# Encoder layer on one core: four regions of the schedule rewritten (opening, rotary tiles of the indexer, branch projections, last blocks)

## The chip, the cores and the metric

The kernel runs on one core of a Trainium2 chip. The metric is the device time of one execution in microseconds (us). Matrix products run on TensorE (PE in the profile), elementwise work on VectorE (DVE), ScalarE (ACT) and GpSimd (POOL); SyncE (SP) issues the transfers. A "split" below writes a float32 tile as a rounded high part (ScalarE) and the remainder as a low part (VectorE or GpSimd); each product is then three matmuls: high by high, high by low, low by high.

## The reference

One layer over 1024 positions of width 1024, in float32. Vectors of shift, scale and gain come from `mod = silu(c) @ w_ada + b_ada`. What is computed, cut to what matters here:

```python
h = rmsnorm(x) * (1 + sc1) + sh1
z = h @ w_in                      # q, k, v of three mixers, an indexer's qi, ki, wi, and the gates
yC: score = sum_h wi * relu(rope(qi_h) @ rope(ki)); top 256 keys per query; attention over them
merged = sum over 3 branches of sigmoid(gate_b) * (y_b @ w_branch[b])
x = x + g1 * rmsnorm(merged @ w_out)
u = gelu(conv(h2 @ w_up_a)) * (h2 @ w_up_g)
x = x + g2 * rmsnorm(u @ w_down)
```

## The kernel before

Positions lie in eight blocks of 128, channels in eight tiles of 128. Outside the parts that are ordered by hand, a planner with a model of the engines sets each engine's order and takes buffers from small pools as they come free; each engine then works strictly in that order. The names of pools are `k4`, `b4`, `e4`, `raw4`, `w4`, `p4` (seven, seven, five, three, four and twelve buffers of 4 KB a partition).

**Opening** (lines 275 to 384, by hand on four engines). SyncE loads the weights of the first modulation pair (`ada_in[0]`), the eight blocks of x, the indexer's weights `raw_qi`, the pair `ada_in[1]`, the keys' weights `raw_kk`, and further pairs. `x_norm(t)` (L299) does a block's square sum on ScalarE, its rsqrt on GpSimd and its scaling on VectorE, all before the next block's. Then for each channel tile k: transposes of x on TensorE (`g0_turn`), modulation and high part on ScalarE (`g0_hi`), low part on GpSimd (`g0_lo`), 18 matmuls into three output tiles (`g0_mm`: two of the indexer's queries, one of keys), while VectorE forms the eight products of the next pair's modulation weights with c (`ada_steps`, 128x256 each, L196, L198). `ada_end` adds the halves, has TensorE sum over the partitions (L208) and writes shift and scale of the next tile (L210), without which `g0_hi` of that tile can't run.

**Rotary tiles** (L394 to L434). `rope` copies a tile out of the banks (ScalarE), has four transfers exchange its halves into `zs`, multiplies z by cos on VectorE (L402), zs by sin on GpSimd (L403) and adds on VectorE (L404): first two query tiles, then the keys' tile. `stack_k` then splits the keys and copies them to the other half of the partitions by transfers (L419, L420); the scores of the indexer (L426, L429) need both copies. Beside this TensorE has 48 matmuls for a mixed tile (L247 to L249, `pm`) and 192 of 128x256 for mixer A's values (L470 to L472), the first of the *fill items*, which the planner sets wherever TensorE would be free. The values' weights are split when the first fill item begins, in `w4` buffers that the mixed tile's weights `wm2` and the indexer's also use.

**Branches** (L992 to L1030). For each branch b and channel tile m, a 128 KB piece of `w_branch` is loaded and split (L1002 to L1004), a gate tile is loaded, 12 matmuls go into two banks of three (L1017 to L1019), VectorE multiplies by the gate (L1021), and for b > 0 GpSimd adds to `M` (L1023). The two y tiles of a branch are loaded and split when the branch begins (L997, L998).

**Last blocks** (L1599 to L1624). The down projection runs in five rounds of seven products into eight banks (`XB`, `VB`), added to `acc` by VectorE (`down_add`, L1643). The last two weight rows are done apart: `final_block(tb)` has 12 matmuls into two banks, and VectorE adds them to `acc` (L1615), ScalarE squares (L1616), GpSimd multiplies by the gain (L1617), then the norm (L1619, L222, L224), and VectorE adds to x (L1623) and SyncE stores. The even blocks go after product 4 of the last round and the odd ones after product 6.

## Time and profile before

| | |
|---|---|
| runs | 1581.08, 1584.87, 1584.56 us; median 1584.56 |
| profiled execution, its own time | 1577.21 us |
| its span | 1575.4 us |
| TensorE, VectorE, ScalarE, GpSimd busy | 95, 73, 50, 36% of the span |

All times of the trace count from the start of the span. An engine's row says in brackets how long it sat idle before the instruction and what released it. The granted clock is a share of TensorE's upper level of 2.4 GHz, so 0.5 is its lower level of 1.2 GHz; a mean between tells how much of a stretch was at either.

### The profile page before, as it was taken

Reading aid. Unit: us, or ns where it says so; the run is one execution under the profiler, and the core shown is the slowest. Engines: PE = TensorE matmul, PEld = TensorE weight load, DVE = VectorE, ACT = ScalarE, POOL = GpSimd, SP = SyncE. Lnnn points to the kernel's source line nnn. Section 1 sums busy time; section 2 is a strip of 40 time slices with the busy share of each in tenths; the row PEclk is TensorE's granted clock in tenths of the full one; section 3 lists DMA queues with packets and bytes.
Section 4 is the critical chain, followed back from the end, with each engine's and each line's share of the span. In section 5 each row is a group of like instructions: output and inputs, shape, how many; then the busy total and the mean of one; then the engine's idle time right before and its main releaser. Section 6 shows DMA issues by size and latency. Waiting matters only on the chain.

```text
span 1575.4 us, 21143 instructions
## 1 busy us (share of the span) xinstructions
PE 1493.3 (95%) x7322; PEld 1234.4 (78%) x7322; DVE 1157.1 (73%) x2106; ACT 787.0 (50%) x1462; POOL 559.6 (36%) x396
## 2 busy tenths in 40 slices
PE   3989999999998999998999989999999999999996
PEld 2878888887887788776888778788888887788885
DVE  6665888998559755557536779888778777879868
ACT  4434698886554444532235455555555554522222
POOL 3632544343443443205542323222223222323305
PEclk9999999999999999999999999999999999999999
DMA  9541332344443452346666412444444445898762
GB/s 287 137 107 47 105 111 84 124 129 131 122 132 90 121 160 88 111 150 204 217 265 215 142 54 94 170 158 166 152 146 164 153 148 173 329 354 293 280 227 108
DMA packets 181727, 253.98 MB, mean 161 GB/s; under 512 B 14891, under 2 KB 132851, under 8 KB 181619
## 3 DMA queue, kind: packets, MB, share of 16 engines
q1 hardware_dynamic: 181619, 252.62, 48.3%
q8 instruction: 58, 0.95, 0.3%
q14 instruction: 50, 0.41, 0.1%
HBM read 169.75 MB, written 74.97 MB: 155 GB/s over the span
## 4 chain that ended last, share of the span: by engine, by line
PE 69%; DVE 15%; DMA 5%; issue 4%; ACT 4%; SPq 2%; POOL 1%; DVEq 0%; POOLq 0%; ACTq 0%
PE g L247 4%; PE g L248 4%; PE X L1268 4%; PE g L249 4%; PE X L1269 4%; PE X L1270 4%; PE X L1632 2%; PE X L1633 2%; PE X L1634 2%; PE V L1268 2%; PE V L1269 2%; PE V L1270 2%; PE V L1632 2%; PE V L1633 2%; PE V L1634 2%
## 5 line engine op out<-in xcount | busy, mean ns | idle before, releaser
L669 ACT ACTIVATE junk<-sc,thr 128x512 bf16<-128x512 f32 (+2 forms) x93 | 80.1, 861 | 25.6 <-DVE thr L690 19.7
L671 DVE TENSOR_SCALAR_CACHE_REDUCE junk<-sc,thr 128x384 bf16<-128x384 f32 (+2 forms) x93 | 89.8, 966 | 1.9
L1234 POOL TENSOR_TENSOR T<-ua 128x512 f32<-128x512 f32 x21 | 27.2, 1294 | 175.7 <-DVE rT L1220 166.1
L1312 POOL TENSOR_TENSOR cv<-cv,g 128x1024 f32<-128x1024 f32 x22 | 57.1, 2598 | 49.3 <-ACT cv L1311 35.4
L1269 PE MATMUL X<-left_S,rT 128*128 128x512 f32 (+1 forms) x184 | 70.8, 385 | 0.2 <-DVE left_S L1114 0.2
L1268 PE MATMUL X<-left_S,rT 128*128 128x512 f32 (+1 forms) x184 | 70.8, 385 | 0.0
L1270 PE MATMUL X<-left_S,rT 128*128 128x512 f32 (+1 forms) x184 | 70.7, 384 | 0.0
L1522 ACT ACTIVATE T<-work 128x512 fp32r<-128x512 f32 x40 | 25.0, 631 | 63.2 <-PE V L1634 26.1
L1235 POOL TENSOR_TENSOR ug<-ug 128x512 f32<-128x512 f32 x22 | 33.0, 1501 | 65.2 <-DVE ua L1228 65.2
L1643 DVE TENSOR_TENSOR acc<-acc,X 128x512 f32<-128x512 f32 x68 | 45.7, 683 | 13.6 <-PE X L1634 13.3
L1023 POOL TENSOR_TENSOR M<-M,tgb 128x1024 f32<-128x1024 f32 x12 | 30.6, 2567 | 66.0 <-DVE tgb L1021 62.2
L585 DVE SCALAR_TENSOR_TENSOR ada_acc<-ada_row,c_act,ada_acc 128x512 f32<-128x512 f32 x42 | 39.3, 936 | 12.9 <-DMA ada_row<-in_w_ada 12.4
L1633 PE MATMUL X<-T,ring 128*128 128x512 f32 x120 | 47.0, 392 | 0.0
L1634 PE MATMUL X<-T,ring 128*128 128x512 f32 x120 | 46.7, 390 | 0.0
L1632 PE MATMUL X<-T,ring 128*128 128x512 f32 x120 | 46.2, 393 | 0.0
L1643 DVE TENSOR_TENSOR acc<-acc,V 128x512 f32<-128x512 f32 x56 | 37.3, 682 | 11.6 <-PE V L1634 11.1
L1220 DVE TENSOR_TENSOR rT<-ua,rT 128x512 fp32r<-128x512 f32 x45 | 38.7, 861 | 9.3 <-ACT rT L1219 9.0
L1219 ACT ACTIVATE rT<-ua 128x512 fp32r<-128x512 f32 x45 | 28.2, 627 | 33.0 <-DVE ua L1232 22.6
L1220 DVE TENSOR_TENSOR rB<-ua,rB 128x512 fp32r<-128x512 f32 x44 | 40.8, 931 | 2.0 <-ACT rB L1219 0.9
L1269 PEld LDWEIGHTS X<-left_S,rT 128*128 128x128 f32 x184 | 34.5, 187 | 8.0 <-DVE left_S L1114 0.4
L1270 PEld LDWEIGHTS X<-left_S,rT 128*128 128x128 f32 x184 | 34.5, 187 | 7.7
L637 DVE SCALAR_TENSOR_TENSOR sc<-rl,wi,sc 128x512 f32<-128x512 f32 (+3 forms) x30 | 30.2, 1038 | 14.0 <-ACT rl L636 14.0
(988 smaller groups left out, 5559.8 us busy)
## 6 DMA issues: line engine op xcount, KB each, us to landing
ring<-L_spill SPq DMA_DIRECT2D x70, 512.0 KB, 6.0
L_spill<-S SPq DMA_DIRECT2D x40, 512.0 KB, 4.0
L_spill<-A SPq DMA_DIRECT2D x30, 512.0 KB, 3.1
raw_g<-in_w_in SPq DMA_DIRECT2D x24, 512.0 KB, 4.1
ada_row<-in_w_ada SPq DMA_DIRECT2D x24, 512.0 KB, 4.0
ua<-in_w_up SPq DMA_DIRECT2D x22, 512.0 KB, 4.3
ug<-in_w_up SPq DMA_DIRECT2D x22, 512.0 KB, 3.9
gate_spill<-tg SPq DMA_DIRECT2D x20, 512.0 KB, 2.7
```

Source lines behind the costliest of these rows:

```text
L247: pe.matmul(o, wh[:, k], hh[:, k, ts_], start=(k == 0), stop=False)
L248: pe.matmul(o, wh[:, k], hl[:, k, ts_], start=False, stop=False)
L669: act.activation(junk_a[:, 0:n], scores[b], AF.Sign, scale=-1.0, bias=t_f, accum_out=cnt[:, j:j + 1])
L671: dve.tensor_scalar(junk_d[:, 0:n], scores[b], t_f, None, op0=OP.is_lt, op1=OP.add, accum_out=cnt[:, j:j + 1])
L1220: eng.tensor_tensor(hl_[1], src, hl_[0].bitcast(F32), op=OP.subtract)
L1268: pe.matmul(oc, r[:, 0, k], lh, start=(first and k == 0), stop=False, skip_group_check=True)
L1269: pe.matmul(oc, r[:, 0, k], ll, start=False, stop=False, skip_group_check=True)
L1270: pe.matmul(oc, r[:, 1, k], lh, start=False, stop=(last and k == 3), skip_group_check=True)
L1632: pe.matmul(o, lh, r[:, 0], start=(starts and k == 0), stop=False, skip_group_check=True)
L1633: pe.matmul(o, lh, r[:, 1], start=False, stop=False, skip_group_check=True)
L1634: pe.matmul(o, ll, r[:, 0], start=False, stop=(k == 1), skip_group_check=True)
L1643: dve.tensor_tensor(dst, dst, banks[i], op=OP.add)
```

## The change

- **Opening.** The square sum and rsqrt of block t now go before the scaling of block t-1; the second weight tile `wqi1` and the pair `ada_in[1]` come on VectorE right after `wqi0`, and the keys' weights are split on GpSimd before the loop over k. From channel tile 2 on, the modulation comes in three *quads* of four column groups (2 MB each, eight transfers, rows of 1 KB in place of 512 B): eight products of 128x512, half of them in each of two steps or all eight in one. `g0_lo` follows `g0_hi`, and at k = 0 the low products of m = 0 and 1 go ahead of the modulation sum.
- **Rotary tiles.** The indexer's three tiles multiply by sin on VectorE too; the order is query tile 0, keys, `stack_k`, query tile 1. `wm2` lies in `b4`. The weights of A's values are loaded and split (high on ScalarE, low on GpSimd) ahead of the rotary tiles.
- **Branches.** `w_branch` comes in six groups of 512 KB, each split in one pair of instructions one group ahead; the y tiles of branch b+1 are loaded at m = 2 and split at m = 4 and 6; those of branch 0 and the first group stand ahead of the loop. `p4` has thirteen buffers.
- **Last blocks.** The last rows' products of the odd blocks' first half and the even blocks' second half are summed in the bank that the down projection still holds, so one VectorE addition does for two; the odd blocks' steps interleave with product 6, by hand on three engines; the very last half is multiplied by the gain on VectorE, all others on GpSimd, as before.

```diff
-N_RAW, N_E, N_K4, N_B4, N_STK, N_PT, N_BI, N_P4 = 3, 5, 7, 7, 4, 2, 1, 12
+N_RAW, N_E, N_K4, N_B4, N_STK, N_PT, N_BI, N_P4 = 3, 5, 7, 7, 4, 2, 1, 13
...
-YG_POOL = (2, 2, 2, 2, 2, 2, 2, 1)
...
+    def ada_quad_load(t, alloc):
+        wv = w_ada.rearrange("(k p) c -> p k c", p=P)
+        raw = [alloc[g](f"ada_quad{t}_{g}", (P, 2, 4 * P)) for g in range(4)]
+        for g in range(4):
+            for j, c in enumerate((t, 8 + t)):
+                nc.sync.dma_start(raw[g][:, :, j * 2 * P:(j + 1) * 2 * P], wv[:, 2 * g:2 * g + 2, c * P:(c + 2) * P])
+        return [raw[k // 2][:, k % 2] for k in range(KD)]
+    def ada_quad_steps(acc, per_k):
+        for k in range(KD):
+            if k == 0:
+                dve.tensor_scalar(acc, per_k[k], c_act[:, k:k + 1], None, op0=OP.mult)
+            else:
+                dve.scalar_tensor_tensor(acc, per_k[k], c_act[:, k:k + 1], acc, op0=OP.mult, op1=OP.add)
+            yield acc
+    def ada_quad_end(t, acc):
+        pm = bank("n", "ada_ps")
+        for j in range(4):
+            pe.matmul(pm[:, j:j + 1], acc[:, j * P:(j + 1) * P], one, start=True, stop=True)
+        for j, c in enumerate((t, t + 1, 8 + t, 9 + t)):
+            last = dve.scalar_tensor_tensor(mod[:, c:c + 1], pm[:, j:j + 1], mod_b1[:, c:c + 1],
+                                            mod_g[:, c:c + 1], op0=OP.add, op1=OP.mult)
+        return last
...
+    quads = {2: ada_quad_load(2, [k4_any] * 4)}
-    for k in range(2, 4):
-        ada_in[k] = ada_load((k, 8 + k), k4_any if k % 2 == 0 else raw4)
+    quads[4] = ada_quad_load(4, [raw4, raw4, raw4, b4])
+    quad_acc = b4("quad_acc", (P, 2, 4 * P))
...
-    def x_norm(t):
-        ss = sm(f"ss{t}")
-        act.activation(junk_a, xn[t], AF.Square, accum_out=ss)
-        r = rstd_of(ss, f"r{t}")
-        dve.tensor_scalar(xn[t], xn[t], r, None, op0=OP.mult)
+    x_r = {}
+    def x_square(t):
+        x_r[t] = sm(f"ss{t}")
+        act.activation(junk_a, xn[t], AF.Square, accum_out=x_r[t])
+    def x_rstd(t):
+        x_r[t] = rstd_of(x_r[t], f"r{t}")
+    def x_scale(t):
+        dve.tensor_scalar(xn[t], xn[t], x_r[t], None, op0=OP.mult)
...
+    quad_of = {}
+    def quad_go(t, n):
+        if t not in quad_of:
+            quad_of[t] = [ada_quad_steps(quad_acc[:, t // 2 % 2], quads[t]), None]
+        for _ in range(n):
+            quad_of[t][1] = next(quad_of[t][0])
     with tc.manual_schedule(engines={E.Activation, E.DVE, E.Pool, E.PE}):
-        for t in range(6):
-            x_norm(t)
-        g0_turn(0, 0)
+        for t in range(NB - 1):
+            x_square(t)
+            x_rstd(t)
+            if t:
+                x_scale(t - 1)
+            if t == 4:
+                g0_turn(0, 0)
-        for t in range(6, NB):
-            x_norm(t)
+        x_square(7)
+        x_rstd(7)
+        x_scale(6)
+        x_scale(7)
-        wqi(1, pool)
+        wqi(1, dve)
+        g0.append(split(raw_kk, (P, KD, P), "wkk", pool, lambda n, sh: f4(n, F32R, sh)))
+        for acc in ada_steps(ada_in[1]):
+            pass
         for k in range(KD):
+                    g0_lo(k, hf)
+            if k == 2:
+                quads[6] = ada_quad_load(6, [k4_any] * 4)
-                steps = ada_steps(ada_in[k + 1])
-                if k:
-                    for n, acc in enumerate(steps):
-                        if n in (3, 5):
-                            g0_lo(k, n // 4)
-                else:
-                    for acc in steps:
-                        pass
-                    g0.append(split(raw_kk, (P, KD, P), "wkk", pool, lambda n, sh: f4(n, F32R, sh)))
-                if k + 4 < KD:
-                    ada_in[k + 4] = ada_load((k + 4, 12 + k), k4_any if k % 2 == 0 else raw4)
-            else:
-                for hf in range(2):
-                    g0_lo(k, hf)
-            if k + 1 < KD:
-                start_end = ada_end((k + 1, 9 + k), acc, eng=dve)
+            if k == 0:
+                g0_mm(k, 0, True)
+                g0_mm(k, 1, True)
+                start_end = ada_end((1, 9), acc, eng=dve)
+                quad_go(2, 4)
+            elif k in (1, 3, 5):
+                if k < 3:
+                    quad_go(k + 1, 4)
+                start_end = ada_quad_end(k + 1, quad_of[k + 1][1])
+            elif k in (2, 4):
+                quad_go(k + 2, 8)
-            for m in range(3):
+            for m in range(2 if k == 0 else 0, 3):
...
-    wm2 = split(raw_m[:, :, 0:72], (P, KD, 72), "wm2")
-    def rope(halves, name, scale, alloc):
+    wm2 = split(raw_m[:, :, 0:72], (P, KD, 72), "wm2", alloc=b4r)
+    def v_weights(c0, name, alloc):
+        ws = []
...
+        return ws
+    va_weights = v_weights(C_VA, "va", w4)
+    def rope(halves, name, scale, alloc, eng=pool):
...
-        pool.tensor_tensor(zs, zs, sin, op=OP.mult)
+        eng.tensor_tensor(zs, zs, sin, op=OP.mult)
...
-    z_qi = [rope(g0_ps[m], f"qi{m}", 1.0, b4) for m in range(2)]
-    z_kk = rope(g0_ps[2], "kk", 1.0, k4)
+    def idx_q(h):
+        return stack_q(b4r, z_qi[h // 2], (h % 2) * 64, f"qi{h}")
+    z_qi = [rope(g0_ps[0], "qi0", 1.0, b4, dve)]
+    z_kk = rope(g0_ps[2], "kk", 1.0, k4, dve)
+    k_idx = stack_k(b4r, z_kk, 64, "ki")
+    z_qi.append(rope(g0_ps[1], "qi1", 1.0, b4, dve))
...
+    def branch_y(b):
+        raws = []
+        for j in range(2):
+            raws.append(k4(f"yb{b}_{j}"))
+            nc.sync.dma_start(raws[j], y_spill[b, j])
+        n_y = iter(range(4))
+        def place(n, sh):
+            i = next(n_y)
+            return p4r(n, sh) if b == 1 and i else e4(n, sh, F32R)
+        def steps():
+            for j in range(2):
+                y_next.append(split(raws[j], (P, S), f"y{b}_{j}", alloc=place))
+                yield
+        return steps()
+    def branch_w(g):
+        rb = raw4(f"wbr{g}", (P, 2, HALF))
+        nc.sync.dma_start(rb, w_branch[g // 2][:, g % 2 * HALF:(g % 2 + 1) * HALF].rearrange("(k p) c -> p k c", p=P))
+        return split(rb, (P, 2, HALF), f"wb{g}", alloc=w4 if g < 4 else p4r)
+    y_next = []
+    for _ in branch_y(0):
+        pass
+    wb_next = branch_w(0)
     for b in range(3):
-        y_s = []
-        for j in range(2):
-            yt = k4(f"yb{b}_{j}")
-            nc.sync.dma_start(yt, y_spill[b, j])
-            y_s.append(split(yt, (P, S), f"y{b}_{j}", alloc=lambda n, sh: e4(n, sh, F32R)))
+        y_s, y_next = y_next, []
         for m in range(KD):
-            wb = p4r(f"wb{b}_{m}", (P, 2, 2, P))
-            rb = raw4(f"wbr{b}_{m}", (P, 2, P))
-            nc.sync.dma_start(rb, w_branch[b][:, m * P:(m + 1) * P].rearrange("(k p) c -> p k c", p=P))
-            act.activation(wb[:, 0], rb, AF.Copy)
-            dve.tensor_tensor(wb[:, 1], rb, wb[:, 0].bitcast(F32), op=OP.subtract)
+            if m % 4 == 0:
+                wb = wb_next
+            elif m % 4 == 1 and (b < 2 or m < 4):
+                wb_next = branch_w(b * 2 + m // 4 + 1)
+            if b < 2:
+                if m == 2:
+                    y_steps = branch_y(b + 1)
+                elif m in (4, 6):
+                    next(y_steps)
+            mc = slice(m % 4 * P, (m % 4 + 1) * P)
...
-    def final_block(tb, banks):
...
+    class Final:
+        def __init__(self, tb):
+            self.tb, self.i, self.odd = tb, tb // 2, tb % 2
+            self.xr = (e4 if tb % 3 else raw4)(f"xf{tb}")
+            nc.sync.dma_start(self.xr, x1_spill[tb * P:(tb + 1) * P, :])
+            self.ss2 = sm(f"n3_{tb}ss2", 2)
+            self.y, self.yg = acc[:, tb], work[:, 4 + self.i]
+        def half(self, e, o, start):
+            for k in range(2):
+                l, r = fin[k][0][self.odd], fin[k][1][e]
+                lh, ll = (l[:, j, self.i * P:(self.i + 1) * P] for j in range(2))
+                pe.matmul(o, lh, r[:, 0], start=(start and k == 0), stop=False, skip_group_check=True)
+                pe.matmul(o, lh, r[:, 1], start=False, stop=False, skip_group_check=True)
+                pe.matmul(o, ll, r[:, 0], start=False, stop=(k == 1), skip_group_check=True)
+            y = self.y[:, es]
+            dve.tensor_tensor(y, y, o, op=OP.add)
+            sq = small.tile([P, HALF], F32, tag="ada_acc", name=f"sq{self.tb}", bufs=1)
+            act.activation(sq, y, AF.Square, accum_out=self.ss2[:, e:e + 1])
+        def gained(self, e):
+            y = self.y[:, es]
+            (dve if e and self.tb == NB - 1 else pool).tensor_tensor(self.yg[:, es], y, G2[e], op=OP.mult)
+        def norm(self):
+            ss = sm(f"n3_{self.tb}ss")
+            dve.tensor_tensor(ss, self.ss2[:, 0:1], self.ss2[:, 1:2], op=OP.add)
+            self.r = rstd_of(ss, f"n3_{self.tb}")
+        def end(self, halves=(0, 1)):
+            tb, xr, r = self.tb, self.xr, self.r
+            for e in halves:
+                es = slice(e * HALF, (e + 1) * HALF)
+                dve.scalar_tensor_tensor(xr[:, es], self.yg[:, es], r, xr[:, es], op0=OP.mult, op1=OP.add)
+                nc.sync.dma_start(out[tb * P:(tb + 1) * P, es], xr[:, es])
...
+                if c == N_C - 1 and n == 4:
+                    final_operands()
+                    evens = [Final(2 * i) for i in range(4)]
+                elif c == N_C - 1 and n == 6:
+                    odds = [Final(2 * i + 1) for i in range(4)]
+                    loads.enter_context(tc.manual_schedule(engines={E.Activation, E.DVE, E.Pool}))
                 for i, _ in enumerate(down_mm(n, next_ops())):
-                    down_add(n, i)
+                    if c < N_C - 1 or n not in (4, 6):
+                        down_add(n, i)
+                    elif n == 4:
+                        evens[i].half(1, VB[i], False)
+                        evens[i].gained(1)
+                    else:
+                        odds[i].half(0, XB[i], False)
+                        if i:
+                            odds[i - 1].norm()
+                        odds[i].gained(0)
+                        odds[i].half(1, VB[i], True)
+                        if i == 3:
+                            odds[3].gained(1)
+                            odds[3].norm()
+                        if i:
+                            odds[i - 1].end()
+                        if i < 3:
+                            odds[i].gained(1)
+                if c == N_C - 1 and n == 6:
+                    odds[3].end()
+                    loads.close()
...
-            if c == N_C - 1:
-                if n == 4:
-                    final_operands()
-                    for i in range(4):
-                        final_block(2 * i, VB[i % 2 * 2:i % 2 * 2 + 2])
-                elif n == 6:
-                    for i in range(4):
-                        final_block(2 * i + 1, (VB if i < 2 else XB)[i % 2 * 2:i % 2 * 2 + 2])
+            if c == N_C - 1 and n == 4:
+                for i in range(4):
+                    evens[i].half(0, VB[i], True)
+                    evens[i].gained(0)
+                    evens[i].norm()
+                    evens[i].end()
```

## Rows read from the trace of the kernel before

**Rows 1.** The page: busy time of the engines over the span, with share and instructions

```profile
PE 1493.3 (95%) x7322; PEld 1234.4 (78%) x7322; DVE 1157.1 (73%) x2106; ACT 787.0 (50%) x1462; POOL 559.6 (36%) x396
```

**Rows 2.** Windows: TensorE, its weight loads, VectorE, ScalarE, GpSimd busy; granted clock; DMA share, GB/s

```profile
26.00:41.00 15.00, 10.29 (x35) 7.70 (x34) 13.61 (x21) 5.13 (x7) 8.88 (x5) 1.00 1.13 264
79.00:125.00 46.00, 39.89 (x247) 34.16 (x246) 28.57 (x31) 16.26 (x28) 14.88 (x5) 0.93 0.36 92
125.00:175.00 50.00, 50.00 (x246) 42.51 (x245) 35.89 (x52) 21.85 (x41) 20.08 (x13) 1.00 0.31 87
175.00:350.00 175.00, 169.44 (x976) 144.98 (x974) 160.33 (x432) 152.88 (x335) 77.30 (x67) 1.00 0.34 102
475.00:525.00 50.00, 43.84 (x219) 35.99 (x220) 48.43 (x90) 20.12 (x40) 18.88 (x13) 0.90 0.30 86
688.00:752.00 64.00, 57.02 (x240) 44.47 (x239) 43.63 (x59) 15.10 (x29) 23.46 (x10) 0.97 0.63 201
1550.00:1575.40 25.40, 13.57 (x60) 10.79 (x58) 19.43 (x35) 5.79 (x16) 11.94 (x12) 0.87 0.34 125
```

**Rows 3.** Timeline, opening: start, length, instructions [idle before, releaser]

```profile
23.46 1.75 DVE L303 TENSOR_SCALAR x<-x,r7r 128x1024 f32<-128x1024 f32 x1 [0.66 <-POOL r7r L224]
25.13 3.38 DVE L232 TENSOR_TENSOR wqi0l<-raw_qi,wqi0h 128x1024 fp32r<-128x1024 f32 x1
28.43 3.74 DVE L196 TENSOR_SCALAR ada_acc<-ada_raw,c_act 128x256 f32<-128x256 f32 x2
...
36.17 0.34 DVE L210 SCALAR_TENSOR_TENSOR mod<-ada_ps,mod_b,mod_g 128x1 f32<-128x1 f32 x2 [1.17 <-PE ada_ps L208]
...
40.85 0.48 PE L333 MATMUL g_0a<-hh,wqi0h 128*128 128x512 f32 x1
```

**Rows 4.** Timeline, TensorE's modulation sums of two successive steps of the opening

```profile
48.28 0.50 PE L208 MATMUL ada_ps<-one,ada_acc 128*128 128x1 f32 x4
...
53.77 0.50 PE L208 MATMUL ada_ps<-one,ada_acc 128*128 128x1 f32 x4
```

**Rows 5.** The page, group: one 128x512 modulation sum on VectorE (count, busy, mean ns)

```profile
L585 DVE SCALAR_TENSOR_TENSOR ada_acc<-ada_row,c_act,ada_acc 128x512 f32<-128x512 f32 x42 | 39.3, 936 | 12.9 <-DMA ada_row<-in_w_ada 12.4
```

**Rows 6.** Waits of TensorE in 20 to 79 us: total, times, longest

```profile
PE ada_ps L208 <- DVE ada_acc L204: 4.0, 2, 3.2
```

**Rows 7.** Waits of TensorE in 79 to 125 us

```profile
PE ix L426 <- DVE qi L412: 3.3, 1, 3.3
PE vaps L471 <- POOL va1l L232: 2.9, 1, 2.9
```

**Rows 8.** Timeline, rotary tiles and first index scores

```profile
84.13 1.23 DVE L402 TENSOR_TENSOR z_qi<-z_qi,cos 128x1024 f32<-128x1024 f32 x1 [6.38 <-DMA zs_qi<-z_qi]
87.66 3.41 DVE L404 TENSOR_TENSOR z_qi<-z_qi,zs_qi 128x1024 f32<-128x1024 f32 x1 [2.31 <-POOL zs_qi L403]
...
98.94 1.23 DVE L404 TENSOR_TENSOR z_kk<-z_kk,zs_kk 128x1024 f32<-128x1024 f32 x1
...
109.46 0.86 PE L429 MATMUL ix<-ki,qi 128*128 128x512 f32 x3
```

**Rows 9.** Waits of TensorE in 688 to 752 us

```profile
PE yp L1017 <- DVE tgb L1021: 3.6, 3, 1.8
PE yp L1017 <- ACT wb L1003: 1.9, 2, 1.4
```

**Rows 10.** Groups in 690 to 752 us: the low parts of the branch weights

```profile
L1004 DVE TENSOR_TENSOR wb<-wbr,wb 128x256 fp32r<-128x256 f32 x20 | 16.5, 832 | 8.9 <-ACT wb L1003 8.9
```

**Rows 11.** Timeline, the tail

```profile
1563.17 0.40 PE L1614 MATMUL X<-wl,ring 128*128 128x512 f32 x1
...
1565.20 0.68 DVE L1615 TENSOR_TENSOR acc<-acc,X 128x512 f32<-128x512 f32 x1
1565.91 1.45 DVE L1617 TENSOR_TENSOR work<-acc,G 128x512 f32<-128x512 f32 x1
...
1570.81 1.41 DVE L1623 SCALAR_TENSOR_TENSOR xf<-work,n_7r,xf 128x512 f32<-128x512 f32 x2 [0.66 <-POOL n_7r L224]
```

## What I predict for the changed kernel

> **What bounds the kernel now.** I read the page first, then windows by stage, then in each stage that the change touches the waits of TensorE and the timeline around them. TensorE is busy 1493.3 of 1575.4 us [rows 1]; the other engines have far more slack over the whole. So only the 82.1 us without a matmul, and stretches at a lowered clock, can be won, as long as TensorE is full afterwards. The windows show where they lie [rows 2]: an unfinished opening (26 to 41: 4.7 us idle), the rotary stretch 79 to 125 (6.1 us idle, mean clock 0.93), the branches 688 to 752 (7.0 us, 0.97), the end. In 125 to 175 TensorE is busy 50.00 of 50 us: what is won before it is passed on and not absorbed there. The profiled execution took 1577.21 us, 7.35 us under the median of the runs; I form the sum as a difference on the trace and take it off the median of 1584.56.
>
> **Opening.** VectorE has the chain. The last scaling of x took 1.75 us, the low part of the first weight tile 3.38 [rows 3], where an operation of that size with nobody beside takes 1.23 [rows 8]: GpSimd was on its own split meanwhile. The change orders the norms so that a block's rsqrt runs under another's scaling (worth 0 to 1.75 us; I take 1.0) and does both weight tiles on VectorE, 2 x 1.23 = 2.5 us. The modulation products then begin at 25.13 - 1.0 + 2.5 = 26.6 in place of 28.43: 1.8 us. Their first two took 3.74 us [rows 3]; a product of twice that width takes 0.94 [rows 5], so unblocked two are at most 1.9. The keys' low part still runs on GpSimd and moves ahead, so of the 1.9 I take 1.5 (0 to 1.9). From the shift and scale at 36.17 to the first matmul of k = 1 at 40.85 there are 4.7 us [rows 3] with ten matmuls and four transposes; four of the ten now go before, about 1.4 (0 to 1.9). That is 4.7 us at k = 1. The steps after it are 53.77 - 48.28 = 5.49 us each [rows 4], TensorE's own work, and stay. Of the two waits for a modulation sum of 4.0 us together the longer, 3.2, is part of this; the other 0.8 [rows 6] was late weights and goes, since quad 6 is asked for at k = 2. Against: the quads. The queue already moves 264 GB/s at a full share (1.13) [rows 2], and 2.1 MB instead of 1.05 MB must land before step k = 2, up to 2.1 / 0.264 - 1.05 / 0.264 = 4.0 us later. On SyncE the bias loads, cos, sin and the mixed tile's weights queue behind eight more issues per quad; their readers come tens of us later, which hides that; without that cover it is the same 4.0. I take 0.5 of the 0 to 4.0. VectorE's work fits: eight products of 0.94 [rows 5] are 7.5 us per two steps of 11.0. Sum: 4.7 + 0.8 - 0.5 = 5.0 us, bounds 0 and 8.
>
> **Rotary tiles and values.** TensorE waits twice in 79 to 125: 2.9 us for the low part of the values' second weight tile, 3.3 us for the indexer's first query split [rows 7]. These are the 6.1 us; the clock of 0.93 adds 7% of 46, 3.2 us [rows 2]. Both waits come out of VectorE and GpSimd sharing a stage: an addition took 3.41 us beside GpSimd's multiplication, and the cos product 1.23 without it [rows 8]. With sin on VectorE the query and keys' tiles are six operations of 1.23: from 84.13 the keys are ready at 91.5 in place of 98.94 + 1.23 = 100.2, 8.7 us sooner, and the second score product, after the same transfers, at about 100.8 instead of 109.46 [rows 8]. Till then TensorE has the mixed tile and the values. The values' splits now stand on GpSimd ahead of the rotary tiles, while VectorE sits idle 6.38 us for the exchange [rows 8]; that hides them, and without it the 2.9 stays. Moving `wm2` costs two of seven `b4` buffers: the copy of query tile 1 out of its banks may wait on ScalarE until tile 0's `zs` is done, 84.13 + 3 x 1.23 = 87.8, and the splits of the keys are queued behind it; they can't begin before 91.5 anyway, so 0 (3.7 at most). The planner writes TensorE's order from modelled times, so I let 1.3 of the second wait and 0.8 of the clock's loss stay: 6.1 + 3.2 - 2.1 = 7.2, taken as 7 us, bounds 2.9 and 9.3.
>
> **Branches.** 7.0 us idle and 3% of 64, 1.9 us, by the clock [rows 2]: 8.9. Of the waits 1.9 us are for a weight's high part and 3.6 for VectorE's emptying of a bank [rows 9]. VectorE's small splits, 20 in this stretch, took 16.5 us, 0.83 each [rows 10]; six of four times the size are 6 x 1.23 alone or 6 x 3.41 beside GpSimd [rows 8], 7 to 20 us, so VectorE gains little and may lose, but they are asked for four tiles ahead. So the 1.9 goes, and most of what I don't have named, while half of the 3.6 and of the clock's 1.9 stays, with 1.0 for the last attention products ahead: 8.9 - 1.8 - 0.9 - 1.0 = 5.2, taken as 5 us, bounds 2 and 8. SyncE loses 18 issues; the y tiles' loads move ahead in its queue by some tiles, past gate loads that are needed later.
>
> **Last blocks.** The last matmul begins at 1563.17 and ends at 1563.57, 11.8 us before the end. The last addition begins only at 1565.20, and after the norm the last pair of results at 1570.81 for 1.41 us [rows 11], 3.2 us before the end: VectorE had four halves queued. With blocks interleaved, behind the last matmul stand an addition (0.68), the gain (1.45), two one-column sums (I estimate 0.3), the former block's pair and the last pair (1.41 each): 5.4, with the 3.2 it is 8.6, so 3.2 us less; 3 taken. The rsqrt on GpSimd hides under the former block's pair. If the gain took 0.68 as an addition does, 4.0 would be won. Eight additions fewer are off the path. Product 4 now needs the last rows' tiles 6 us or so sooner; no row shows when these land, so 0, with up to 1.5 as bound. Bounds 1 and 4.
> The gain took 1.45 us with a multiplication on GpSimd beside it [rows 11]. The Trainium skill, "SBUF — State Buffer", section "Who interferes with whom", says that a VectorE instruction with two SBUF inputs and a GpSimd one that reads SBUF shut each other out for a whole instruction; the row agrees. It speaks against this part, for GpSimd keeps fifteen of sixteen gains while VectorE's pairs move beside them: with one more such block behind the last matmul the saving would be about 2 us instead of 3.
>
> **Sum.** 5 + 7 + 5 + 3 = 20 us: the profiled execution would go from 1577.2 to 1557.2, the median from 1584.6 to 1564.6.
>
> **Rivals.**
> *The planner keeps the waits.* Rotary stretch and branches are not ordered by hand: if the scores stand as early in TensorE's order as now, or the banks are emptied as late, only opening and tail remain, 8 us: 1576.6. For it: both waits of rows 7 are of an order that time did not bear out. Against: four causes of waits go from the data's side. Chance 0.17.
> *Given back later.* In 175 to 350 VectorE is busy 160.3 of 175 us [rows 2]; if the search for thresholds there, and not TensorE, sets when attention can go on, what opening and rotary tiles win becomes idle time of TensorE: 8 us from branches and tail, 1576.6. Against: TensorE has 169.4 of 175, and the scores come earlier as well. Chance 0.07.
> *Slower.* In 475 to 525 VectorE is full (48.43 of 50), TensorE idles 6.2 us and the clock of 0.90 takes 5.0: 11.2 us per 50 [rows 2]. The planner's new times reorder the 500 us of fill behind the opening. If 175 to 350 became like that, it would lose 3.5 x 11.2 - 5.6 (idle already) = 33.6 us: 1598. It decides from the point at which VectorE lacks its 14.7 us of slack there, that is, fill items used up before. Against: the change adds no VectorE work after 100 us, and the rates that hand out fill are as they were. Chance 0.05.
>
> **How the numbers follow.** The forecast holds with 0.66, 1551 to 1572; 0.05 for still more (all upper ends: 1555, with a lucky reorder less). Opening, rotary, branches and tail at their lower ends, 0 + 2.9 + 2 + 1, give 1578.7. The range 1550 to 1578 takes in the forecast and most of the first two rivals. A measurement tells about 0.3% from no change, 4.8 us: faster than 1579.8 are the forecast, the better case and most of the two rivals, 0.89; 0.06 within, 0.05 slower.
>
> **What would show it.** Right: the first matmul of k = 1 near 36, the opening's end some 5 us earlier, no wait for a modulation sum over 1 us; the rotary stretch without the values' wait, and scores 13 us earlier with the opening's 5; six weight splits in the branches and under 4 us idle; less than 9 us behind the last matmul. Wrong: a wait for quad weights at k = 2, sin products slower than 1.3 us, or new idle time of TensorE over 10 us between 125 and 688, which would be the planner's and overturn the sum.

## The result, and the profile after

The median of the runs is 1568.01 us after (1564.69 to 1569.83) against 1583.85 before (1581.08 to 1584.87); the ratio is 0.9902, 95% interval 0.9883 to 0.9921. The forecast of 1564.6 was 3.4 us too low, and faster was right: 20 us were forecast, 15.8 came. But the parts of the sum did not come as they were forecast: the branches gave more, the last blocks nothing, the opening nothing against its own profile, and the stretch behind the rotary tiles took some back. The profiled execution of after took 1564.69 us (span 1562.6), 12.5 less than that of before.

Part 1 of the page of after (busy time, share, instructions):

```profile
PE 1490.3 (95%) x7322; PEld 1233.8 (79%) x7322; DVE 1131.3 (72%) x2054; ACT 783.4 (50%) x1444; POOL 547.9 (35%) x392
```

TensorE's time without a matmul fell from 82.1 to 72.3 us. A table by stage shows where the rest lies. The marks are first matmuls before which the same work has been done in each kernel (but for two matmuls of some 1240 at the first mark): mixer A's third score tile (`A2s`), mixer C's last (`C3s`), the output projection (`wo`) and the down projection (`X`).

| from the profiles, us | before | after | after - before |
|---|---|---|---|
| start to A2s (opening, rotary tiles, scores) | 260.4 | 251.7 | -8.7 |
| A2s to C3s (search, attention, gates) | 384.9 | 388.4 | +3.5 |
| C3s to wo (branches) | 164.8 | 156.1 | -8.7 |
| wo to X | 101.6 | 102.0 | +0.4 |
| X to the end | 663.7 | 664.4 | +0.7 |

The stretches of after that answer to [rows 2] (stretch, its length, then busy time and count of each engine, granted clock, DMA share, GB/s):

```profile
25.00:41.00 16.00, 12.75 (x43) 9.72 (x42) 14.62 (x19) 5.29 (x7) 6.80 (x4) 0.79 0.99 302
79.00:125.00 46.00, 45.21 (x298) 39.73 (x297) 29.03 (x49) 19.50 (x32) 9.54 (x4) 1.00 0.40 104
674.00:752.00 78.00, 76.54 (x358) 63.07 (x357) 43.33 (x58) 21.49 (x28) 33.68 (x14) 1.00 0.58 200
```

The rotary stretch and the branches are full at the full clock; the opening is not. TensorE's waits in the second and third of these stretches, all of them, in answer to [rows 7] and [rows 9] (total, times, longest):

```profile
PE ix L485 <- DVE sc L683: 0.5, 1, 0.5
PE vaps L525 <- ACT va L528: 0.3, 1, 0.3
...
PE yp L1096 <- DVE M L1100: 0.8, 1, 0.8
PE yp L1097 <- DVE y_1l L258: 0.7, 1, 0.7
```

The opening of after, in answer to [rows 3] (start, duration; in brackets the idle time before and what ended it):

```profile
26.80 1.64 DVE L195 TENSOR_SCALAR ada_acc<-ada_raw,c_act 128x256 f32<-128x256 f32 x2
28.36 4.56 DVE L197 SCALAR_TENSOR_TENSOR ada_acc<-ada_raw,c_act,ada_acc 128x256 f32<-128x256 f32 x6
29.46 2.38 POOL L258 TENSOR_TENSOR wkkl<-raw_kk,wkkh 128x1024 fp32r<-128x1024 f32 x1 [1.44 <-ACT wkkh L257]
...
33.52 0.98 PE L207 MATMUL ada_ps<-one,ada_acc 128*128 128x1 f32 x4 [3.22 <-DVE ada_acc L203]
...
34.54 0.34 DVE L209 SCALAR_TENSOR_TENSOR mod<-ada_ps,mod_b,mod_g 128x1 f32<-128x1 f32 x2 [1.17 <-PE ada_ps L207]
...
35.31 7.29 DVE L233 SCALAR_TENSOR_TENSOR quad_acc<-ada_quad,c_act,quad_acc 128x512 f32<-128x512 f32 x7
...
38.63 0.71 PE L366 MATMUL g_0a<-hh,wqi0h 128*128 128x512 f32 x1
...
42.75 1.02 PE L239 MATMUL ada_ps<-one,quad_acc 128*128 128x1 f32 x8 [1.78 <-DVE quad_acc L233]
...
46.82 0.48 PE L366 MATMUL g_0a<-hh,wqi0h 128*128 128x512 f32 x1
```

The first row shows the products beginning at 26.80, as worked out (26.6). The next two show GpSimd's split of the keys beside the six later products, which take 4.56 us. TensorE waits 3.2 us for their sum as it did before, its next matmuls take 0.63 to 0.78 us in place of 0.39, and k = 1 begins at 38.63. Then it waits 1.8 us for the first quad, and k = 2 begins at 46.82, later than the 46.34 of before.

The rotary chain of after, in answer to [rows 8], and the view of the tile with the second score product (min/median/max ns, first and last start):

```profile
90.32 1.23 DVE L461 TENSOR_TENSOR z_qi<-z_qi,cos 128x1024 f32<-128x1024 f32 x1 [18.06 <-DMA zs_kk<-z_kk]
...
96.24 1.22 DVE L463 TENSOR_TENSOR z_kk<-z_kk,zs_kk 128x1024 f32<-128x1024 f32 x1
...
L488 PE MATMUL ix<-ki,qi x15: 280/393/397, 104.9 to 125.8; 128*128 128x512 f32 x10, 128*128 128x384 f32 x3, 128*128 128x256 f32 x1, 128*128 128x128 f32 x1
```

Every operation takes 1.2 us, as forecast, but VectorE begins at 90.32 and not at 84.13. The row names the keys' exchange as what ended the wait, but the last transfer of that lands only at 92.4; the first query tile's, which the operation needs, lands at 90.1. The first score product begins at 104.7 us (104.27 before) and the second kind at 104.9 (109.46 before), 4.6 us sooner where 13 had been named as the sign. The last blocks, in answer to [rows 11]:

```profile
1549.84 2.96 POOL L1705 TENSOR_TENSOR work<-acc,G 128x512 f32<-128x512 f32 x2
1549.90 3.44 DVE L1716 SCALAR_TENSOR_TENSOR xf<-work,n_3r,xf 128x512 f32<-128x512 f32 x2
...
1550.72 0.40 PE L1695 MATMUL V<-wl,ring 128*128 128x512 f32 x1
1553.26 0.67 DVE L1698 TENSOR_TENSOR acc<-acc,X 128x512 f32<-128x512 f32 x1
...
1554.82 1.77 DVE L1705 TENSOR_TENSOR work<-acc,G 128x512 f32<-128x512 f32 x1
...
1556.78 1.41 DVE L1716 SCALAR_TENSOR_TENSOR xf<-work,n_5r,xf 128x512 f32<-128x512 f32 x2
```

When the last matmul runs, VectorE is in a pair of results that takes 3.44 us beside GpSimd's two gains (the same pair without GpSimd: 1.41, last row). Behind the last matmul stand 1562.6 - 1551.12 = 11.5 us; before it was 11.8.

### The profile page after: what moved, and what is told of

The parts are those of the page before. It is cut to its first block, busy times and chain, and to the rows that moved or that the text cites. A ratio compares the mean times of both kernels' runs of the same rounds, so it can differ in the third digit from the quotient of the medians.

```text
span 1562.6 us, 20978 instructions
## 1 busy us (share of the span) xinstructions
PE 1490.3 (95%) x7322; PEld 1233.8 (79%) x7322; DVE 1131.3 (72%) x2054; ACT 783.4 (50%) x1444; POOL 547.9 (35%) x392
## 4 chain that ended last, share of the span: by engine, by line
PE 66%; DVE 17%; DMA 5%; ACT 5%; issue 4%; SPq 2%; POOL 0%; DVEq 0%; ACTq 0%; POOLq 0%
PE X L1347 4%; PE X L1348 4%; PE X L1349 4%; PE g L273 3%; PE g L275 3%; PE g L274 3%; PE X L1725 2%; PE X L1726 2%; PE X L1727 2%; PE V L1347 2%; PE V L1348 2%; PE V L1349 2%; PE V L1725 2%; PE V L1726 2%; ACT junk L719 2%
## 5 line engine op out<-in xcount | busy, mean ns | idle before, releaser
L1601 ACT ACTIVATE T<-work 128x512 fp32r<-128x512 f32 x40 | 25.0, 631 | 63.8 <-PE V L1727 26.6
L1348 PEld LDWEIGHTS X<-left_S,rT 128*128 128x128 f32 x184 | 34.5, 187 | 8.0 <-DVE left_S L1193 0.4
L1349 PEld LDWEIGHTS X<-left_S,rT 128*128 128x128 f32 x184 | 34.4, 187 | 7.7
L1347 PEld LDWEIGHTS X<-left_S,rT 128*128 128x128 f32 x184 | 34.5, 187 | 7.5
```

The lines of the kernel that those rows point to most:

```text
L1347: pe.matmul(oc, r[:, 0, k], lh, start=(first and k == 0), stop=False, skip_group_check=True)
L1348: pe.matmul(oc, r[:, 0, k], ll, start=False, stop=False, skip_group_check=True)
L1349: pe.matmul(oc, r[:, 1, k], lh, start=False, stop=(last and k == 3), skip_group_check=True)
```

## The experiments

Each group of kernels ran on one chip beside the kernel before, whose medians were 1582.7 (the four parts), 1582.1, 1584.1 and 1579.0 us; ratios are to these. The stages of all their profiles stand in a table at the end of this section.

**Each part alone**, on the kernel before; the edit is that part of the diff above.

> The opening's edits alone, all else as before. Prediction on record: -5.0 us (bounds 0 to 8), so 1578.9 by the median of 1583.85. Theory now, from the trace of the changed kernel: the first matmul of k = 1 moves from 40.85 to 38.6 (2.2 us), then TensorE waits 1.8 us for the first quad, whose eight products VectorE can only begin at 34.8; little is left, 0 to 1.5 us, so 1582.4 to 1583.9 as far as the opening itself goes. Rival: the wait for the quad is made good later in the opening by the shorter steps (5.0 in place of 5.5 us) and 4 to 5 us stay, 1579 to 1580. For the middle (190 to 640 us): if it gives back a share of what is won ahead of it, nearly nothing is lost here; if the planner's order just falls differently, the middle moves by some us either way, whatever was won.

Measured: 1580.47, ratio 0.9981 (0.9968 to 0.9994), so -3.0 us. Neither theory nor rival: against the profile of before nothing is won at A2s (260.2 against 260.4), and yet the median falls. The other three traces point to the reason. Their opening is the code of before, but its last matmul begins at 84.0, 83.9 and 87.4 us (the last with matmuls of the mixed tile set into the opening), not at 78.7. The same step in the trace of the kernel with the last blocks alone, and then in that of before:

```profile
45.25 4.54 DVE L197 SCALAR_TENSOR_TENSOR ada_acc<-ada_raw,c_act,ada_acc 128x256 f32<-128x256 f32 x6
...
46.43 3.07 POOL L322 TENSOR_TENSOR hl<-h,hh 128x512 fp32r<-128x512 f32 x2 [4.59 <-ACT hh L318]
...
50.39 0.58 PE L207 MATMUL ada_ps<-one,ada_acc 128*128 128x1 f32 x4 [0.80 <-DVE ada_acc L203]
56.93 0.58 PE L207 MATMUL ada_ps<-one,ada_acc 128*128 128x1 f32 x4 [0.81 <-DVE ada_acc L203]
```

```profile
44.09 2.46 DVE L198 SCALAR_TENSOR_TENSOR ada_acc<-ada_raw,c_act,ada_acc 128x256 f32<-128x256 f32 x6
...
45.27 3.84 POOL L323 TENSOR_TENSOR hl<-h,hh 128x512 fp32r<-128x512 f32 x2 [3.28 <-ACT hh L319]
...
60.60 4.54 DVE L198 SCALAR_TENSOR_TENSOR ada_acc<-ada_raw,c_act,ada_acc 128x256 f32<-128x256 f32 x6
...
65.74 0.58 PE L208 MATMUL ada_ps<-one,ada_acc 128*128 128x1 f32 x4 [0.81 <-DVE ada_acc L204]
```

In one execution VectorE is held up, in the other GpSimd; the step is 6.54 or 5.49 us long. The profile on which the prediction rests shows the second course in four of five such steps and the first in one (its last two lines), and it lay 5.5 and 7.35 us under the two medians of before (1582.71, 1584.56). Against an opening of the first course throughout (A2s at 266.0) the opening's edits win 5.8 us, of which 2.8 go again between A2s and C3s. That the runs without a profile mostly go the first course is argued from these traces, not shown.

> The rotary tiles' and values' edits alone. Prediction on record: -7 us (2.9 to 9.3), 1576.9. Theory now: the stretch from 79 to 125 us wins about 8 us of the 8.7 that the changed kernel is ahead when mixer A's scores stand at the same work (194.0 against 187.6 us, and 227.0 against 218.4), and the middle gives 2 to 4 us of it back, so the whole is -4 to -6, 1578 to 1580. Rival one (the middle's loss belongs to this part's order alone and grows or falls by chance): more than 2 us off that. Rival two (the lead in the changed kernel came from the opening): the lead here at mixer A's scores is 4 us or less.

Measured: 1585.15, ratio 1.0015 (0.9999 to 1.0031): no gain, rather +2.4 us. The theory's lead is there (A2s at 256.4 against 266.0 with the same opening, -9.6), but it is all given back, against the kernel with the last blocks alone: +4.2 between A2s and C3s (389.1 against 384.9), +3.8 in the old branches, +1.8 in the last rounds. Rival two is out; rival one fits the size. Why the branches and the last rounds, whose code here is that of before, took longer is not shown.

> The branches' edits alone. Prediction on record: -5 us (2 to 8), 1578.9. Theory now: the changed kernel's lead grew by 8.7 us between 640 and 810 us (from 5.2 to 13.9), where no other edit acts, so this part alone gives -8 to -9, 1575 to 1576, with TensorE idle under 1 us from the first branch matmul to the last and everything before 640 us as in the kernel before, if the planner's order there is not touched. Rival: part of the 8.7 us came from the other order of the work before it, and alone it gives the 5 that were predicted, 1579.

Measured: 1572.25, ratio 0.9931 (0.9912 to 0.9951), so -10.9 us (-7.8 to -13.9). The theory holds: C3s to wo takes 156.2 us, as in every kernel that has this part (156.1 or 156.2 in eight traces); without it that stretch is 163.8 to 167.6, and longest with the rotary edits. TensorE still waits 1.5 us from the first branch matmul to the last, a little more than the 1 us expected.

> The last blocks' edits alone. Prediction on record: -3 us (1 to 4), 1580.9. Theory now: behind the last matmul VectorE still has a pair of results that takes 3.44 us beside GpSimd's two gain products, where a pair without GpSimd takes 1.41; the time from the last matmul's end to the span's end falls only from 11.8 to 11.5 us, so -0.4, 1583.5, and with up to 1 us more of TensorE's own time in the last rounds -0.4 to +0.7. Rival: the changed kernel's end was a single bad overlap and alone the part gives its 3 us, with 8.6 to 9 us behind the last matmul.

Measured: 1582.47, ratio 0.9995 (0.9981 to 1.0009). The theory holds: X to the end is 664.9 us, where the kernels with the old end have 663.7 to 666.7. The four alone add up to -12.3 us, together they measured -15.5 by the ratio; the intervals are too wide to call that a difference.

**The last blocks without GpSimd's gains**, on the kernel after.

```diff
-            (dve if e and self.tb == NB - 1 else pool).tensor_tensor(self.yg[:, es], y, G2[e], op=OP.mult)
+            (dve if self.odd else pool).tensor_tensor(self.yg[:, es], y, G2[e], op=OP.mult)
```

> The changed kernel, but the gain products of all four odd blocks on VectorE instead of GpSimd (seven more there). Theory: VectorE and GpSimd hold each other up: a pair of results takes 3.44 us beside GpSimd's gains and 1.41 alone. Then a block costs VectorE 2 x 0.68 + 2 x 0.7 + 0.3 + 1.41 = 4.5 us against 4.1 of TensorE (18 matmuls of 0.227), and behind the last matmul remain some 4.5 us of VectorE and 3.1 of the store: 7.5 to 8 us in place of 11.5, so -3.5 to -4 us, 1564 to 1564.5. Rival: a gain product costs VectorE 1.45 to 1.77 us, as the one it has now does, whoever runs beside it; then a block costs 6 us, VectorE falls 2 us behind with every block, and the end comes 2 us later, 1570.

```profile
1551.66 1.41 DVE L1716 SCALAR_TENSOR_TENSOR xf<-work,n_3r,xf 128x512 f32<-128x512 f32 x2
...
1553.05 0.40 PE L1695 MATMUL V<-wl,ring 128*128 128x512 f32 x1
...
1555.76 0.69 DVE L1705 TENSOR_TENSOR work<-acc,G 128x512 f32<-128x512 f32 x1
```

A gain is 0.69 us and a pair 1.41: the rival is out. Behind the last matmul stand 9.2 us in place of 11.5, not the theory's 7.5 to 8, and X to the end is 661.9, 2.5 less. The whole was 1565.75, ratio 0.9895 (0.9882 to 0.9908), which can't be told from after: its trace lost 1.9 us between A2s and C3s.

**The keys' split off GpSimd**, on the kernel after: the split before the loop is gone, and `ada_end((1, 9))` is written out with the split inside.

```diff
-                start_end = ada_end((1, 9), acc, eng=dve)
+                dve.tensor_tensor(acc[:, 0], acc[:, 0], acc[:, 1], op=OP.add)
+                ... (the two sums on TensorE)
+                g0.append(split(raw_kk, (P, KD, P), "wkk", dve, lambda n, sh: f4(n, F32R, sh)))
+                ... (shift and scale)
```

> The changed kernel, but the low part of the keys' weights comes from VectorE, between the addition that ends the pair (1, 9) and the shift and scale of k = 1, instead of from GpSimd beside the eight products of that pair. Theory: beside GpSimd's 2.38 us the six later products took 4.56 us, unhindered 2.46, so the modulation sum stands 2 to 3 us earlier (30.4 to 31.4 in place of 33.4), TensorE's wait of 3.2 us at 30.3 shrinks to 0 to 1 and its clock doesn't fall again; the first matmul of k = 1 comes at 35 to 36.5 in place of 38.6, the wait for the first quad stays near 2 us, and 2 to 3 us are left at the opening's end. Total -1 to -3 us, 1565 to 1567, if the middle passes it on. Rival: the products are slowed by the transfers (290 GB/s between 30 and 40 us), not by GpSimd; then they still take 4.5 us, the split of 1.2 us comes on top, and k = 1 begins no earlier, 1568 to 1569.

```profile
28.63 2.46 DVE L197 SCALAR_TENSOR_TENSOR ada_acc<-ada_raw,c_act,ada_acc 128x256 f32<-128x256 f32 x6
...
34.79 0.48 PE L366 MATMUL g_0a<-hh,wqi0h 128*128 128x512 f32 x1
...
40.79 1.02 PE L239 MATMUL ada_ps<-one,quad_acc 128*128 128x1 f32 x8 [3.28 <-DVE quad_acc L233]
...
46.47 0.47 PE L366 MATMUL g_0a<-hh,wqi0h 128*128 128x512 f32 x1
```

The six products take 2.46 us beside the same transfers, so it was GpSimd; k = 1 begins 3.8 us sooner. But the wait for the first quad grows from 1.8 to 3.3 us, so its sum begins only 2.0 us sooner (40.79 for 42.75): the quad ends last. And k = 2 is no more than 0.35 sooner, because from that sum to k = 2 TensorE now takes 5.7 us for 4.1, at a granted clock of 0.71 from 40.7 to 46.5. Median 1565.78, ratio 0.9892 (0.9879 to 0.9906), which can't be told from after either.

**The low parts of h on VectorE**, on the kernel before.

```diff
-        pool.tensor_tensor(hl[:, k, hs], h32[k][:, hs], ...)
+        (dve if k else pool).tensor_tensor(hl[:, k, hs], h32[k][:, hs], ...)
```

> The kernel before, but with the low parts of h (128x512, two per step, k from 1) on VectorE instead of GpSimd. In the profile of before a step of the opening took 5.49 us, with six products of 128x256 in 2.46; in the profiles of the kernels with the branches alone and with the last blocks alone, whose opening is the same code, it took 6.53, the six products 4.54, and the opening ended 5.2 us later. Theory: that is VectorE and GpSimd taking turns, and in most executions VectorE loses; without GpSimd there the products take 2.46 in every execution, a step is TensorE's 5.5 to 5.7 us, and the opening ends near 79 to 80 in place of 84: 3 to 5 us off the median, 1578 to 1580 (some of it may be given back in the middle). Rival: the products are slow because weights land late or beside transfers; then six still take 4.5 us, VectorE has 1.4 us more per step, and the kernel is 5 us or more slower, 1588 or more.

Measured: two products take 0.87 us in every step, the opening ends at 79.0 in place of 84, and A2s begins at 261.7 in place of 266.0: in the traces it is GpSimd that holds VectorE up, and the rival is out. The median did not follow: 1581.19, ratio 0.9991 (0.9980 to 1.0002), some 1.4 us where the theory had 3 to 5. Either the runs of before often go the shorter course as well, or later stretches take the gain back. The profiled execution was the fastest of its kernel (1576.64), so its trace can't show which; this stays open.

**Grouped weights alone**, on the kernel before (the y tiles as they were, when a branch begins).

> The kernel before with the branches' grouped weights alone: the y tiles of a branch are loaded and split where they were, when the branch begins. The whole part measured -10.9 us (0.9931), with 7.5 us won between the first and the last branch matmul. Theory: the waits in the branches are for the weights' high parts and for VectorE, which the 20 small splits burden (16.5 us), so the groups carry most of it: -6 to -9 us, 1574 to 1577. Rival: the y tiles, which hold up the first matmuls of each branch, are half of it or more: -2 to -5 us, 1578 to 1581, with waits for y tiles at the start of branches 1 and 2 of 1 us or more each.

Measured: 1574.51, ratio 0.9949 (0.9937 to 0.9961), -8.1 us; C3s to wo 158.4 us. The theory holds: the groups carry most, the y tiles ahead some 2 us by the trace.

**The first quad in halves**, on the kernel with the keys' split on VectorE: eight products over the columns of tile 2, then eight over those of tile 3, each ended by its own sums.

```diff
-                quad_go(2, 4)
+                quad_go(2, 8)
...
+            elif k == 1:
+                quad_go(2, 4)
+                start_end = ada_quad_end(2, quad_of[2][1], (0, 2))
+                quad_go(2, 4)
+                quad_go(4, 2)
...
```

> The kernel with the keys' split on VectorE, and of the first quad the columns for channel tile 2 are formed first (eight products of 128x256 over half the width), those for tile 3 after them; two products of the second quad go ahead. Measured there: k = 1 begins at 34.79 in place of 38.63, but TensorE then waits 3.3 us for the whole quad (7.8 us of VectorE) and its clock falls, so k = 2 begins at 46.47 in place of 46.82. Theory: the whole quad is what ends last. Eight half products at 0.41 are 3.3 us, ready at 36.5, before TensorE asks at 37.3; the wait goes, k = 2 begins at 40.5 to 42.5, and the opening ends 3 to 6 us earlier than in the changed kernel; the start of mixer A's second scores (218.4) moves to 213 to 216. By the median -2 to -5, if the middle passes on what it is given. Rival: the quads' loads land late; then a wait of 2 us or more stays at k = 1 or 2 and the opening gains under 1 us.

```profile
32.97 5.42 DVE L245 SCALAR_TENSOR_TENSOR quad_acc<-ada_quad,c_act,quad_acc 128x256 f32<-128x256 f32 x7
...
38.53 0.58 PE L251 MATMUL ada_ps<-one,quad_acc 128*128 128x1 f32 x4 [1.29 <-DVE quad_acc L245]
...
42.75 0.48 PE L380 MATMUL g_0a<-hh,wqi0h 128*128 128x512 f32 x1
...
52.36 1.02 PE L251 MATMUL ada_ps<-one,quad_acc 128*128 128x1 f32 x8 [1.81 <-DVE quad_acc L233]
```

The theory of what ends last holds: k = 2 begins 4.1 us sooner than in after, A2s 2.4. Seven half products took 5.42 us beside GpSimd's low parts, not 2.9, and the second quad is late in its turn. The median shows nothing of it: 1566.78 (1560.15 to 1571.80), ratio 0.9899 (0.9878 to 0.9921).

**The keys first in the planner**, on the kernel after.

```diff
+    with tc.high_priority(200):
         z_qi = [rope(g0_ps[0], "qi0", 1.0, b4, dve)]
         z_kk = rope(g0_ps[2], "kk", 1.0, k4, dve)
         k_idx = stack_k(b4r, z_kk, 64, "ki")
```

> The changed kernel, with the indexer's first query tile and keys (rotary operations, split and copies) given a higher priority in the planner; nothing else. In TensorE's order the scores then stand at matmul 390 to 722 of the program, in place of 399 to 741 (before: 330 to 683). Question: why the stretch from mixer A's second scores to mixer C's last is 421.7 to 423.9 us in all kernels that have the rotary edits and 414.0 to 421.2 in those without. Theory: the scores stand some 60 matmuls later in TensorE's order, so the search for thresholds on VectorE starts later against TensorE's work, and VectorE has 11 us more to do beside mixer A's and B's attention (132.7 against 121.7 us in the stretch that takes 142 against 137); a third of that shift undone gives 1 to 3 us in the middle, 1565 to 1567. Rival: the middle's length follows other details of the order; then it changes by more than 3 us or in the wrong direction.

Measured: 1562.26 (1561.10 to 1563.09), ratio 0.9863 (0.9844 to 0.9882), below after's interval. A2s to C3s is 384.8 us, 3.6 less than in after and shorter than in any of the six traces that have after's order there (386.3 to 392.1). (The expectation's mark, mixer A's second scores, can't serve: the priority moved them 32 matmuls earlier.) The theory holds in direction; but more came than the 1 to 3 it promised, and more than 3 was the rival's sign, so the rival is not out. The stretch in question, A2s to mixer B's second scores, of before, of after, of the rotary edits alone and of this kernel, and after's waits in it:

```profile
260.40:397.00 136.60, 129.91 (x695) 108.48 (x695) 121.70 (x318) 110.33 (x237) 55.93 (x46) 1.00 0.40 125
```

```profile
251.70:394.00 142.30, 133.39 (x700) 111.13 (x699) 132.73 (x342) 116.26 (x249) 57.53 (x49) 0.98 0.39 119
```

```profile
256.40:398.60 142.20, 133.49 (x698) 110.88 (x697) 132.76 (x342) 116.08 (x249) 57.30 (x49) 0.98 0.38 119
```

```profile
252.20:392.00 139.80, 132.01 (x698) 110.40 (x696) 128.78 (x335) 114.11 (x246) 56.08 (x47) 0.99 0.39 122
```

```profile
PE A3y L872 <- DVE A3pl L889: 2.1, 1, 2.1
PE kB L273 <- ACT z_qB L548: 1.9, 2, 1.6
PE B0s L488 <- DMA Bk<-Bk: 1.8, 1, 1.8
PE A2s L485 <- DVE A2m L834: 1.6, 2, 1.0
```

For nearly the same matmuls (five more) VectorE is busy 11 us more in after than in before. The rotary edits alone come to that stretch 4.7 us later and show the same counts. Over all profiles, the six kernels with after's order take 142.1 or 142.2 us for it, whenever they come to it (249.3 to 256.4 us); the six with the order of before take 136.4 to 138.2, the two with the priority 139.8. It is the order that does it, not the moment of arrival. That the later scores are the reason is argued, not shown: the priority moved other work too.

**Together.** First opening and last blocks, then all three mendings.

> The kernel with the first quad in halves and the keys' split on VectorE, and with the gain products of the odd last blocks on VectorE. If opening (-2 to -5) and last blocks (-2.5 by the trace, from the first down product to the end 661.9 in place of 664.4 us) add up, the median is 1561 to 1564 and lies under both kernels. Rival: an end that waits for VectorE in every block (3.97 us a block) and an opening whose gain the middle takes back: 1565 to 1568, no better than the changed kernel.

Measured: 1564.19 (1559.60 to 1568.90), ratio 0.9878 (0.9857 to 0.9898); X to the end 662.3, but A2s to C3s 392.1. The interval holds the theory and the rival, and the kernel can't be told from after (0.9902) nor from either part alone. Its opening is that of the kernel with the quad in halves, but A2s begins at 253.0 and not at 249.3. The step from the first half quad's sum to k = 2 in that kernel, then in this one:

```profile
38.50:42.80 4.30, 3.89 (x23) 3.10 (x23) 4.09 (x11) 2.17 (x4) 0.72 (x1) 1.00 0.93 293
```

```profile
38.90:44.80 5.90, 5.44 (x23) 4.27 (x23) 5.65 (x12) 2.71 (x4) 2.27 (x2) 0.71 0.92 303
```

Behind a wait of 1.3 us in both, the step takes 4.2 us there (38.53 to 42.75) and 5.8 here (38.98 to 44.79), at a mean granted clock of 1.00 or 0.71; a wait of 0.4 us for the shift is part of the difference. The second quad's step differs by 1.6 us again. So this opening too comes out differently in executions of the same code, here 3.7 us at A2s, which may be why its gain doesn't show in the medians.

> All three mendings together on the changed kernel: keys' split on VectorE and the first quad in halves (opening), the indexer's first query tile and keys at a higher priority, the gain products of the odd last blocks on VectorE. Alone they measured 0.9899, 0.9863 and 0.9895 of before (the changed kernel 0.9902). If they add as the traces show them (mixer A's second scores 3.2 us earlier, the middle some 3 us shorter, the last rounds 2.5 us shorter), the ratio is 0.983 to 0.986, some 1557 to 1562 us. Rival: the middle takes back what the opening gives and only the priority counts, 0.986 to 0.988.

Measured: 1555.19 (1553.48 to 1560.27), ratio 0.9861 (0.9839 to 0.9884). It is faster than before, and by the ratios than after too (0.0041 lower, give or take 0.003 from the two intervals), though those two did not run beside each other. The priority alone has 0.9863; the interval holds the theory's upper end and the rival, so the opening's and the end's share can't be told in the whole. The stages of the profiles, us:

| kernel | start to A2s | A2s to C3s | C3s to wo | X to end |
|---|---|---|---|---|
| opening alone | 260.2 | 387.7 | 164.1 | 665.0 |
| rotary alone | 256.4 | 389.1 | 167.6 | 666.7 |
| branches alone | 267.0 | 384.0 | 156.2 | 665.4 |
| last blocks alone | 266.0 | 384.9 | 163.8 | 664.9 |
| low parts on VectorE | 261.7 | 380.5 | 165.8 | 665.2 |
| grouped weights alone | 266.1 | 381.8 | 158.4 | 664.2 |
| gains on VectorE | 252.5 | 390.3 | 156.1 | 661.9 |
| keys' split on VectorE | 250.7 | 390.6 | 156.2 | 663.9 |
| quad in halves | 249.3 | 386.3 | 156.2 | 664.6 |
| keys first | 252.2 | 384.8 | 156.1 | 664.6 |
| opening and last blocks | 253.0 | 392.1 | 156.2 | 662.3 |
| all three | 247.2 | 384.1 | 156.2 | 662.4 |

## Why the prediction was right, and where it was wrong

**The base.** The step that failed first is a sentence ahead of the sum: the profiled execution lay 7.35 us under the median, and I carried the difference over as if it belonged to no place. By the traces some 5 us of it have one: in that execution VectorE won four of its five turns against GpSimd in the opening. "The steps after it are 53.77 - 48.28 = 5.49 us each [rows 4], TensorE's own work, and stay" was not true even there. One step took 6.46 us, and its wait of 0.8 us, which I put down to late weights, came when VectorE's six products took 4.54 us beside GpSimd. In four other profiles with the same code all five steps took 6.5, and in the three where nothing else stands in the opening it ended 5.2 to 5.5 us later. That the total came out near is in part luck: the parts were 7.5 us too large (20 against 12.5 between the profiles), and the base hid 3.3 of the 15.8 us that the medians show.

**Opening, -5.0.** Against its own profile the opening won nothing (260.2 against 260.4 alone). The chain to the products was right (26.80 against 26.6). "Of the 1.9 I take 1.5": zero came, the lower bound. GpSimd's split moved, but only from beside the first two products to beside the six: 6.57 us from the first product to the sum in both kernels. "Four of the ten now go before, about 1.4": 4.09 against 4.68 us, 0.6, since all six that stayed took 0.63 to 0.78 us (granted clock 0.50 from 34.3 to 38.6, the lower of the two levels), while the last four of the ten of before took 0.39 to 0.41. The granted clock does not tell all: in before it is 1.00 from 36 to 39, and four matmuls there took 0.63 to 0.78 as well. And "VectorE's work fits", eight products or 7.5 us per two steps, is wrong for the first quad, which can begin only at 34.80 and so has the time of one step; the wait is VectorE's 7.8 us of products without a gap, not late transfers, and it took the remaining 2.2 us.

**Rotary tiles, -7.** Both waits went and the clock is 1.00, so the stretch won what it held: 9.6 us at A2s, just above the upper bound. The path was not the one described. The planner set matmuls of the mixed tile into the opening's end, the last of the opening's own begins at 82.4, the first query tile's exchange lands at 90.1, and the keys are ready at 97.5, not 91.5. The scores came no earlier in TensorE's order but later, 69 matmuls at their first and 58 at their last (399 to 741 in place of 330 to 683 by the count of the recorded expectation). That is the part of the rivals that came true, in another shape than either: the waits were not kept, but with the new order 4 to 6 us are given back between A2s and mixer B's second scores (142.2 us in place of 136.4 to 138.2). From A2s to C3s only 3.5 of it show, because the profile of before has there a wait of 2.7 us for `Bb` that is 0.4 in after (last section). One row was misread on the way: the product of 1.23 us at 84.13 was not "without" GpSimd, whose multiplication began 0.03 us behind it and took 3.48; VectorE was the first there, not alone. The size holds: the same operations took 1.2 us in after.

**Branches, -5.** Right in mechanism, and mis-sized: 8.7 us by the trace. I let half of the 3.6, half of the clock's loss and 1.0 of the attention products stay; nearly all of it went, 1.5 us of waits remain, and the stretch has become the same length in every kernel whatever comes before it.

**Last blocks, -3.** Wrong. "Behind the last matmul stand an addition" overlooked that VectorE would be one pair behind, held up by the two gains of the block before: 3.44 for 1.41, and the gain 1.77. The prediction had named that rule and still priced it at 1 us for one block; it applied to all. Without GpSimd there the same steps leave 9.2 us behind the last matmul, near the 8.6 of the sum (its terms as listed make 5.25 and not 5.4, so 8.45).

So -5, -7, -5, -3 became, by the profiles, -8.7 for the first two, +3.5 behind them, -8.7, and +1.1 for the rest.

## What to carry to other kernels

Ask of a profiled execution that is faster than the median where it was faster, before taking differences on its trace. Where VectorE and GpSimd work beside each other on the path, price every operation of either at both ends, alone and held up, and look at what the moved one will stand beside next. A gain ahead of a stretch that a planner orders is worth what is left behind it: compare marks of equal work, not times.

## What the runs showed of the hardware

Sixty nanoseconds decide over 2.3 us. In after VectorE's write of 128x384 began 0.06 us ahead of GpSimd's split, in the kernel with the gains on VectorE 0.13 us behind it (the two fences, in this order):

```profile
468.64 0.35 DVE L770 TENSOR_SCALAR sc<-junk 128x384 f32<-128x384 bf16 x1
468.70 2.56 POOL L258 TENSOR_TENSOR wg_2l<-raw_g,wg_2h 128x1024 fp32r<-128x1024 f32 x1 [3.30 <-ACT wg_2h L257]
```

```profile
469.47 2.47 POOL L258 TENSOR_TENSOR wg_2l<-raw_g,wg_2h 128x1024 fp32r<-128x1024 f32 x1 [3.20 <-ACT wg_2h L257]
469.60 2.56 DVE L770 TENSOR_SCALAR sc<-junk 128x384 f32<-128x384 bf16 x1
```

In six of the fourteen profiles, that of before among them, that operation took 2.6 us, and TensorE then waited 2.7 or 2.8 us for a score tile (`Bb`) in place of 0.3 to 0.5. (In the run with the quad in halves VectorE's recorded start is 0.02 us behind GpSimd's and it still took 0.35; differences that small the record doesn't order.) The opening shows such an order falling differently in executions of the same code, 5 us apart, and within one execution from step to step; if it does so here, this place is 2.3 us more of the up to 13 us by which runs of one kernel lie apart. Which other places there are was not tried. The Trainium skill, "SBUF — State Buffer", section "Who interferes with whom", says that whoever issues first keeps the shared ports for a whole instruction and that not the shape but the order decides who waits; these rows agree.
